# Residual block in float32 by split products: the "added" pair of a column block begun one pair ahead, and six, then eight seven-product pairs in the down projection

## Chip, cores, metric

The kernel runs on 1 core of one Trainium2 chip. The metric is the device time of one execution in microseconds. Three timed executions of the kernel before gave 1150.38, 1150.60 and 1150.38 us.

## What is computed

One layer over 256 tokens of width 2048, all in float32: a combined input projection, chunked softmax attention in eight heads, a gated recurrence (HGRN2) in eight heads, an output projection, and a SwiGLU block of inner width 5632. The change lies in the last part:

```python
    x = x + (mixed @ w_out[l]).astype(x.dtype)
    h2 = rmsnorm(x, norm2_gain[l])
    ff = jax.nn.silu(h2 @ w_gate[l]) * (h2 @ w_up[l])
    x = x + (ff @ w_down[l]).astype(x.dtype)
return rmsnorm(x, final_gain)
```

## The kernel before

**Split products.** A float32 product is made of three products in float32r: each operand is split in a high and a low half (`split`, L87: ScalarE copies to the high half, L88, and VectorE subtracts it from the source for the low half, L89), and TensorE forms high by high, high by low and low by high (`mul`, L699, matmul at L704). Weights are split on the chip as they arrive; high halves stand in tiles `wh`, low halves in `wl`, each a pool of four buffers.

**Pairs.** Gate and up are computed in 11 groups of 512 columns each (`Gated`, list `gated`), down in two groups (`Down`). A group goes over its contraction in pairs of 128-row blocks. Of each pair the four weight tiles (two row blocks by two outputs) come in one load of 1024 KB, and a pair is prepared (`prepare`) in one of three ways:

- `"d"`, ordinary: two halves of 128x1024 are split by ScalarE and VectorE, then 24 matmuls of 512 columns.
- `"s"`, seven-product: sums and differences of the tiles `ta` and `tb` are formed on VectorE (L747 to L749) and split too, so that seven instead of eight block products do, 21 matmuls. The sums of the left operand stand ready in `hs` (gate and up) or `sf` (down, made by `row_sums` from `fh` and `fl`).
- `"a"`, added: VectorE does nothing. `begin` (L711) loads the pair to `rawa` (one buffer), ScalarE writes its negated high half to `low` (L716, two halves of 128x1024, three buffers), and a DMA on GpSimd's queue adds the weights from memory onto it (L717), which leaves the low half. `prepare_begun` (L722) makes the high halves `wh` on ScalarE. Its 24 matmuls take the 16 with high halves first, and the 8 with `low` last.

A gated group after the first has the order of L879, `a4 s0 d5 s1 a6 s2 s3 d7`: 4 x 24 + 4 x 21 = 180 matmuls, and 8 transposes of 128x128. Group 0 has ordinary pairs alone. The last pair of a group is held and run output block by output block, so that VectorE and ScalarE can take each block as it ends.

**Order of work.** `run_groups` (L773) calls `prepare(i + 1)` and then runs the matmuls of the pair before it, so one pair is prepared while another runs; the order on each engine is settled by the scheduler from there. `prepare` also decides when an added pair begins: two pairs ahead if an ordinary pair comes between (a4 of the next group begins with s3), one pair ahead if a seven-product pair is followed by it (a6 begins with s1). All plain loads go through one queue, SP's, in program order (`dma`, L81, chains them): a load that waits for its buffer holds all that follow. Ordinary and seven-product pairs share three buffers `raw`.

**Down.** `order_of` (L765) lists a down group: some ordinary pairs first, then seven-product pairs with an ordinary one behind each, then the ordinary ones that are left. Group 0 has 7 ordinary pairs, 7 seven-product pairs with 6 ordinary ones between them, and 2 ordinary pairs at the end; group 1 has 1, then 8 seven-product pairs with ordinary ones between, and ordinary ones at the end. While the first ordinary pairs of group 0 run, `between` (L942) has `row_sums` make the four tiles of sums (each serves two seven-product pairs). Behind the last seven-product pair `spread` (L903) adds the products m1, m5, m6, m7 into the residual `x2`; behind the group `block` (L919) and `end` (L937) add and scale the output blocks.

Of the kernel before, what the change touches and what calls it, by code (L numbers as in the profile page):

```python
# [8 lines left out]
F32 = mybir.dt.float32  # L9
F32R = mybir.dt.float32r  # L10
I32 = mybir.dt.int32
AF = mybir.ActivationFunctionType
# [33 lines left out]
def hybrid_block(ctx: ExitStack, tc: tile.TileContext, x, xT, w_in, w_out, w_gu, w_down,  # L46
# [616 lines left out]
    def row_sums(dst, hi, lo):  # L663
        n = hi.shape[1] // 2
        a = dn.tile([P, 2, 2, S], F32, tag="ta", name="a")[:, 0:n]
        sm = dn.tile([P, 4, 2, P], F32, tag="tb", name="sm")[:, :, 0:n]
        nc.vector.tensor_tensor(a, hi.rearrange("p (j k) t -> p j k t", k=2).bitcast(F32),
                                lo.rearrange("p (j k) t -> p j k t", k=2).bitcast(F32), ALU.add)
        a11, a12, a21, a22 = a[:, :, 0, 0:P], a[:, :, 1, 0:P], a[:, :, 0, P:S], a[:, :, 1, P:S]
        nc.vector.tensor_tensor(sm[:, 0], a21, a22, ALU.add)  # L670
        nc.vector.tensor_tensor(sm[:, 1], sm[:, 0], a11, ALU.subtract)
        nc.vector.tensor_tensor(sm[:, 2], a11, a21, ALU.subtract)
        nc.vector.tensor_tensor(sm[:, 3], a12, sm[:, 1], ALU.subtract)
        split(dst[:, 0], dst[:, 1], sm)
# [8 lines left out]
    class Group:  # L683
# [25 lines left out]
            return load_chunk(self.src, self.base + j).rearrange("p (b n) -> p b n", n=W)  # L709

        def begin(self, j):  # L711
            raw, low = own["low"].tile([P, 4, W], F32, name="rawa"), []
            dma(raw.rearrange("p b n -> p (b n)"), self.src[self.base + j])
            for k in range(2):
                wl = own["low"].tile([P, 2, W], F32R, tag="low", name="low", bufs=3)
                tc.keep_in_program_order(nc.scalar.activation(wl, raw[:, 2 * k:2 * k + 2], AF.Copy, scale=-1.0))  # L716
                nc.gpsimd.dma_start(out=wl.rearrange("p b n -> p (b n)"),  # L717
                                    in_=self.src[self.base + j, :, 2 * k * W:2 * (k + 1) * W], accum_op=ALU.add)
                low.append(wl)
            self.begun = raw, low  # L720

        def prepare_begun(self, j):  # L722
            (raw, low), self.begun = self.begun, None
            tiles = []
            for k in range(2):
                wh = wsp.tile([P, 2 * W], F32R, tag="wh", name="wh")
                nc.scalar.activation(wh, raw[:, 2 * k:2 * k + 2].rearrange("p b n -> p (b n)"), AF.Copy)
                tiles.append([(wh[:, i * W:(i + 1) * W], low[k][:, i]) for i in range(2)])
            return [(f"c{t}{h}", self.lhs(2 * j + k, t), tiles[k][h if k == 0 else 1 - h], terms)
                    for terms in ((0, 2), (1,)) for k in range(2) for t in range(NT) for h in range(2)]  # L730
# [34 lines left out]
    def order_of(pairs, fast, lead, tail):  # L765
        slow = [j for j in range(pairs) if j not in fast]
        items = [("d", j) for j in slow[:lead]]
        mid = slow[lead:len(slow) - tail]
        for n, j in enumerate(fast):
            items += [("s", j)] + [("d", k) for k in mid[n:n + 1]]  # L770
        return items + [("d", j) for j in mid[len(fast):] + slow[len(slow) - tail:]]

    def run_groups(groups, following=None):  # L773
        todo = [(gr, n) for gr in groups for n in range(len(gr.items))]

        def prepare(i):
            kinds = [gr.items[n][0] for gr, n in todo[i:i + 3]]
            ahead = 2 if kinds[1:] == ["d", "a"] else 1 if kinds[0] == "s" and kinds[1:2] == ["a"] else 0
            if ahead:
                gr, n = todo[i + ahead]  # L780
                gr.begin(gr.items[n][1])
            gr, n = todo[i]
            return gr.prepare(*gr.items[n])

        steps, held = groups[0].ready or prepare(0), []
        for i, (gr, n) in enumerate(todo):
            ahead = None
            if n + 1 == len(gr.items):
                if i + 1 < len(todo):
                    ahead = prepare(i + 1)  # L790
                elif following is not None:
                    following.ready = following.prepare(*following.items[0])
                gr.run_blocks(held + steps, gr.block)
                held = []
                gr.end()
            elif n + gr.hold >= len(gr.items):
                held = held + steps
            else:
                gr.run(steps)
                seen = sum(1 for kind, _ in gr.items[:n + 1] if kind == "s")  # L800
                if gr.items[n][0] == "s" and seen == gr.ns:
                    gr.spread()
            if i + 1 < len(todo):
                steps = ahead or prepare(i + 1)
            gr.between(n)
# [28 lines left out]
    class Gated(Group):  # L834
# [31 lines left out]
        def between(self, n):  # L866
            if n == 0:
                if self.g == 0:
                    second_end()
                    for t in range(NT):  # L870
                        dma(x2d[t], x2[:, t, :])
                    own["hs"] = res.tile([P, 2, 4, FASTU, P], F32R, tag="res", name="hs")
                else:
                    ff_split(gated[self.g - 1].ff, self.g - 1)
            if self.g == 0 and 1 <= n <= (FASTU + 1) // 2:
                j0, j1 = 2 * n - 2, min(2 * n, FASTU)
                row_sums(own["hs"][:, :, :, j0:j1, :], h2[:, 2 * j0:2 * j1, 0, :], h2[:, 2 * j0:2 * j1, 1, :])
# [19 lines left out]
    class Down(Group):  # L897
# [39 lines left out]
        def end(self):  # L937
            if self.g == 0:
                for t, h in BLOCKS:
                    self.gained(t, h)  # L940

        def between(self, n):  # L942
            if self.g == 0:
                if n == 0:
                    gup.__exit__(None, None, None)
                    late = ctx.enter_context(tc.tile_pool(name="late", bufs=1))
                    own.update(f_last=late.tile([P, 2, 4, S], F32R, name="f_last"), fg=late.tile([P, D], F32, name="fg"))
                    ff_split(gated[-1].ff, len(gated) - 1)
                elif n <= FAST // 2:
                    ks = slice(4 * (n - 1), 4 * n)  # L950
                    row_sums(sf[:, n - 1], fh[:, ks, :], fl[:, ks, :])
                elif n == FAST // 2 + 1:
                    load_fg()
                if n == 2:
                    x2 = own["x2"] = res.tile([P, NT, D], F32, tag="res", name="x2")
                    for t in range(NT):
                        dma(x2[:, t, :], x2d[t])

    def finish(ps, t):
# [6 lines left out]
        for lo, hi in ((c0, c1), (c1, D)):  # L966
# [18 lines left out]
        nc.scalar.activation(x2[:, t, 1024:c0], x2[:, t, 1024:c0], AF.Copy, scale=r)  # L985
        dma(out[t, :, 1024:c0], x2[:, t, 1024:c0])

    down = [Down(g, order_of(KP, list(range(FAST - 1 + g)), 1 if g else 7, 2), w_down, g * KP, f_of, s_of)
            for g in range(2)]
    down[0].hold, down[1].hold = 1, 2  # L990
    run_groups(gated, down[0])
# [63 lines left out]
```

## Time and profile before

| | us |
|---|---|
| timed runs (3), median | 1150.38 |
| the profiled execution's own time | 1149.81 |
| its span, first to last instruction | 1148.1 |
| TensorE matmul busy (PE) | 1132.1 |
| TensorE weight load busy (PEld) | 943.9 |
| VectorE busy (DVE) | 914.5 |
| ScalarE busy (ACT) | 700.1 |

Times are of one profiled execution. The profile calls SyncE's queue SP and GpSimd POOL; "SPq" is a queue's issue of a DMA. A row of the view by windows gives a stretch, its length, and for each engine the busy time and the number of instructions. A row of the view in order of time gives start, duration, engine, line and operands, and in brackets how long the engine stood idle before it and what ended that. Matmuls overlap, so the time from one start to the next says more of TensorE's pace than the duration of one.

### The profile page before, as it was taken

Reading aid. Unit: us, or ns where it says so; the run is one execution under the profiler, and the core shown is the slowest. Engines: PE = TensorE matmul, PEld = TensorE weight load, DVE = VectorE, ACT = ScalarE, POOL = GpSimd, SP = SyncE. Lnnn points to the kernel's source line nnn. Section 1 sums busy time; section 2 is a strip of 40 time slices with the busy share of each in tenths; the row PEclk is TensorE's granted clock in tenths of the full one; section 3 lists DMA queues with packets and bytes.
Section 4 is the critical chain, followed back from the end, with each engine's and each line's share of the span. In section 5 each row is a group of like instructions: output and inputs, shape, how many; then the busy total and the mean of one; then the engine's idle time right before and its main releaser. Section 6 shows DMA issues by size and latency. Waiting matters only on the chain.

```text
span 1148.1 us, 14308 instructions
## 1 busy us (share of the span) xinstructions
PE 1132.1 (99%) x5381; PEld 943.9 (82%) x5381; DVE 914.5 (80%) x1166; ACT 700.1 (61%) x900; POOL 53.2 (5%) x73
## 2 busy tenths in 40 slices
PE   9999999999999999999999999999999999999996
PEld 7888888888888888888888788788788888878885
DVE  7577768947746666589889889889889998899885
ACT  7465656846645555576676676676676565555553
POOL 3200000000000000010010010010010000000000
PEclk9999999999999999999999999999999999999999
DMA  9655544554744547877886886886887765546552
GB/s 330 229 196 185 179 147 179 180 192 147 279 161 154 189 172 281 259 209 208 293 242 211 290 241 215 291 237 220 283 237 245 269 231 204 200 175 236 189 214 74
DMA packets 41397, 248.95 MB, mean 217 GB/s; under 512 B 4848, under 2 KB 5360, under 8 KB 15344
## 3 DMA queue, kind: packets, MB, share of 16 engines
q1 hardware_dynamic: 35568, 227.06, 53.5%
q0 software_dynamic: 5760, 20.97, 10.2%
q8 instruction: 42, 0.69, 0.2%
q14 instruction: 27, 0.22, 0.1%
HBM read 243.82 MB, written 4.19 MB: 216 GB/s over the span
## 4 chain that ended last, share of the span: by engine, by line
PE 87%; DVE 5%; ACT 3%; DMA 2%; issue 2%; ACTq 0%; SPq 0%; DVEq 0%
PE c L704 40%; PE acc L169 10%; PE m L704 10%; PE acc L171 5%; PE acc L144 5%; PE acc L146 5%; PE acc L145 5%; DVE wl L89 2%; ACT wh L88 2%; PE vps L144 1%; PE vps L145 1%; PE vps L146 1%; PE ptr L315 1%; DMA raw<-in_w_gu_dram 1%; DMA raw<-in_w_down_dram 1%
## 5 line engine op out<-in xcount | busy, mean ns | idle before, releaser
L89 DVE TENSOR_TENSOR wl<-raw,wh 128x1024 fp32r<-128x1024 f32 (+1 forms) x378 | 419.0, 1124 | 140.6 <-ACT wh L88 139.8
L88 ACT ACTIVATE wh<-raw 128x1024 fp32r<-128x1024 f32 (+1 forms) x378 | 362.1, 972 | 205.3 <-PE acc L146 75.2
L704 PE MATMUL c<-wh,h 128*128 128x512 f32 x928 | 277.0, 391 | 1.7 <-ACT wh L88 1.7
L704 PEld LDWEIGHTS c<-wh,h 128*128 128x128 f32 x928 | 173.5, 188 | 40.8 <-ACT wh L88 5.2
L169 PE MATMUL acc<-hx,wh 128*128 128x512 f32 x512 | 179.7, 395 | 0.0
L171 PE MATMUL acc<-hx,wl 128*128 128x256 f32 x512 | 142.6, 278 | 0.0
L704 PE MATMUL c<-wl,h 128*128 128x512 f32 x304 | 118.4, 389 | 0.2 <-DVE wl L89 0.2
L169 PEld LDWEIGHTS acc<-hx,wh 128*128 128x128 f32 x512 | 96.0, 188 | 21.7
L88 ACT ACTIVATE wh<-ta 128x1024 fp32r<-128x1024 f32 x55 | 58.3, 1061 | 73.6 <-DVE ta L747 34.9
L88 ACT ACTIVATE wh<-tb 128x1024 fp32r<-128x1024 f32 x55 | 58.3, 1060 | 63.0 <-PE c L704 32.6
L171 PEld LDWEIGHTS acc<-hx,wl 128*128 128x128 f32 x512 | 96.4, 188 | 0.1
L704 PE MATMUL c<-wh,fh 128*128 128x512 f32 x230 | 89.7, 390 | 0.2 <-DVE ff L853 0.2
L704 PE MATMUL c<-wh,fl 128*128 128x512 f32 x230 | 89.5, 389 | 0.0
L704 PE MATMUL c<-wl,fh 128*128 128x512 f32 x230 | 89.5, 389 | 0.0
L704 PE MATMUL m<-wh,hs 128*128 128x512 f32 x240 | 83.0, 392 | 1.3 <-ACT wh L88 1.3
L89 DVE TENSOR_TENSOR wl<-tb,wh 128x1024 fp32r<-128x1024 f32 x55 | 67.3, 1223 | 21.2 <-ACT wh L88 20.0
L89 DVE TENSOR_TENSOR wl<-ta,wh 128x1024 fp32r<-128x1024 f32 x55 | 67.2, 1222 | 15.0 <-ACT wh L88 14.9
L747 DVE TENSOR_TENSOR ta<-raw 128x1024 f32<-128x1024 f32 x55 | 67.3, 1223 | 10.6 <-DMA raw<-in_w_gu_dram 6.9
L717 POOL DMA_DIRECT2D low<-in_w_gu_dram x40 | 34.5, 871 | 730.5 <-ACT low L716 690.5
L704 PEld LDWEIGHTS c<-wl,h 128*128 128x128 f32 x304 | 57.1, 188 | 12.6 <-DVE wl L89 0.6
L704 PEld LDWEIGHTS m<-wh,hs 128*128 128x128 f32 x240 | 45.0, 188 | 12.8 <-ACT wh L88 3.7
L704 PEld LDWEIGHTS c<-wh,fh 128*128 128x128 f32 x230 | 43.2, 188 | 9.4 <-issue 0.6
(289 smaller groups left out, 1848.3 us busy)
## 6 DMA issues: line engine op xcount, KB each, us to landing
raw<-in_w_gu_dram SPq DMA_DIRECT2D x68, 1024.0 KB, 8.2
raw<-in_w_in_dram SPq DMA_DIRECT2D x48, 1024.0 KB, 4.8
raw<-in_w_down_dram SPq DMA_DIRECT2D x44, 1024.0 KB, 4.8
rawa<-in_w_gu_dram SPq DMA_DIRECT2D x20, 1024.0 KB, 5.2
low<-in_w_gu_dram POOLq DMA_DIRECT2D x40, 512.0 KB, 8.6
raw<-in_w_out_dram SPq DMA_DIRECT2D x16, 1024.0 KB, 4.8
raw<-in_w_in_dram SPq DMA_DIRECT2D x12, 512.0 KB, 6.0
raw<-in_w_in_dram SPq DMA_DIRECT2D x8, 256.0 KB, 4.6
```

Source lines behind the costliest of these rows:

```text
L88: nc.scalar.activation(hi, src, AF.Copy)
L89: nc.vector.tensor_tensor(lo, src, hi.bitcast(F32), ALU.subtract)
L144: nc.tensor.matmul(ps[t], lhsT=xh[:, tok], rhs=wh, start=kt == 0, stop=False)
L145: nc.tensor.matmul(ps[t], lhsT=xh[:, tok], rhs=wl, start=False, stop=False)
L146: nc.tensor.matmul(ps[t], lhsT=xl[:, tok], rhs=wh, start=False, stop=kt == kts - 1)
L169: nc.tensor.matmul(ps[m].rearrange("p j t -> p (j t)"), lhsT=wh[:, col], rhs=both, start=kt == 0, stop=False)
L171: nc.tensor.matmul(ps[m][:, 0, :], lhsT=wl[:, col], rhs=rhs[:, kt, 0, :], start=False, stop=kt == KD - 1)
L315: nc.tensor.transpose(pt[:, j, t, :], nat(t)[:, n0 + j * P:n0 + (j + 1) * P], ident)
L704: nc.tensor.matmul(self.bank[n], lhsT=a, rhs=b, start=self.left[n] == self.total[n], stop=self.left[n] == 1)
L717: nc.gpsimd.dma_start(out=wl.rearrange("p b n -> p (b n)"), in_=self.src[self.base + j, :, 2 * k * W:2 * (k + 1) * W], accum_op=ALU.add)
L747: nc.vector.tensor_tensor(ta, raw[:, 1:3], raw[:, 0:2], ALU.subtract)
```

## The change

Three things change.

1. An added pair begins always exactly one pair ahead. `begin` is cut in two: it loads `rawa`, and a new function `lower(k)` negates one half and issues its adding DMA. Ahead of a seven-product pair (a6 before s1) both halves come first, as they did. Ahead of an ordinary pair (a4 before d7 of the group ahead) the load and half 0 stand before that pair's own load and splits, and half 1 behind them; before, all of it stood ahead of s3, one pair earlier.
2. Down group 0 has 6 seven-product pairs in place of 7: 6 ordinary pairs, then six seven-product pairs each with an ordinary one behind it, then 4 ordinary ones. Its number of matmuls grows by 3. Group 1 keeps its order (8 seven-product pairs).
3. Only three tiles of sums are made in down group 0. The fourth is made in group 1, after its fifth pair; the load of the final gain comes one pair earlier.

```diff
         def begin(self, j):
-            raw, low = own["low"].tile([P, 4, W], F32, name="rawa"), []
+            raw = own["low"].tile([P, 4, W], F32, name="rawa")
             dma(raw.rearrange("p b n -> p (b n)"), self.src[self.base + j])
-            for k in range(2):
-                wl = own["low"].tile([P, 2, W], F32R, tag="low", name="low", bufs=3)
...
-            self.begun = raw, low
+            self.begun = j, raw, []
+
+        def lower(self, k):
+            j, raw, low = self.begun
+            wl = own["low"].tile([P, 2, W], F32R, tag="low", name="low", bufs=3)
+            tc.keep_in_program_order(nc.scalar.activation(wl, raw[:, 2 * k:2 * k + 2], AF.Copy, scale=-1.0))
+            nc.gpsimd.dma_start(out=wl.rearrange("p b n -> p (b n)"),
+                                in_=self.src[self.base + j, :, 2 * k * W:2 * (k + 1) * W], accum_op=ALU.add)
+            low.append(wl)
...
         def prepare(i):
-            kinds = [gr.items[n][0] for gr, n in todo[i:i + 3]]
-            ahead = 2 if kinds[1:] == ["d", "a"] else 1 if kinds[0] == "s" and kinds[1:2] == ["a"] else 0
-            if ahead:
-                gr, n = todo[i + ahead]
-                gr.begin(gr.items[n][1])
             gr, n = todo[i]
-            return gr.prepare(*gr.items[n])
+            nxt, m = todo[i + 1] if i + 1 < len(todo) else (None, 0)
+            begins = nxt is not None and nxt.items[m][0] == "a"
+            if begins:
+                nxt.begin(nxt.items[m][1])
+                nxt.lower(0)
+                if gr.items[n][0] == "s":
+                    nxt.lower(1)
+            steps = gr.prepare(*gr.items[n])
+            if begins and gr.items[n][0] == "d":
+                nxt.lower(1)
+            return steps
...
+        def sum_round(self, i):
+            ks = slice(4 * i, 4 * i + 4)
+            row_sums(sf[:, i], fh[:, ks, :], fl[:, ks, :])
+
         def between(self, n):
+            if self.g == 1 and n == 4:
+                self.sum_round(FAST // 2 - 1)
...
-                elif n <= FAST // 2:
-                    ks = slice(4 * (n - 1), 4 * n)
-                    row_sums(sf[:, n - 1], fh[:, ks, :], fl[:, ks, :])
-                elif n == FAST // 2 + 1:
+                elif n < FAST // 2:
+                    self.sum_round(n - 1)
+                elif n == FAST // 2:
                     load_fg()
...
-    down = [Down(g, order_of(KP, list(range(FAST - 1 + g)), 1 if g else 7, 2), w_down, g * KP, f_of, s_of)
+    down = [Down(g, order_of(KP, list(range(FAST if g else FAST - 2)), 1 if g else 6, 2), w_down, g * KP, f_of, s_of)
```

What stands on the engines, at the end of one gated group and the start of the next. On SP's queue before, from the load of s2 of one group to that of s0 of the next:

```order
L85 DMA raw_4389<-in_w_gu_dram 128x2048
L85 DMA rawa_4433<-in_w_gu_dram 128x2048
L85 DMA raw_4441<-in_w_gu_dram 128x2048
L85 DMA raw_4492<-in_w_gu_dram 128x2048
L85 DMA raw_4566<-in_w_gu_dram 128x2048
```

Here 4389 is s2, 4433 a4, 4441 s3, 4492 d7, 4566 s0. In the changed kernel the same place reads s2 (4389), s3 (4433), a4 (4484), d7 (4489), s0 (4566):

```order
L85 DMA raw_4389<-in_w_gu_dram 128x2048
L85 DMA raw_4433<-in_w_gu_dram 128x2048
L85 DMA rawa_4484<-in_w_gu_dram 128x2048
L85 DMA raw_4489<-in_w_gu_dram 128x2048
L85 DMA raw_4566<-in_w_gu_dram 128x2048
```

The load of s3 and that of a4 have changed places.

On ScalarE before, from the last split of s2 (wh<-tb, first row) to the high halves of a4 (wh<-rawa); the copy ff<-m begins the group's spread:

```order
L88 ACTIVATE wh<-tb 128x1024
L716 ACTIVATE low<-rawa 128x1024 x2
L88 ACTIVATE wh<-raw 128x512
L88 ACTIVATE wh<-raw 128x1024
L88 ACTIVATE wh<-ta 128x1024
L842 COPY ff<-m_4603 128x512
L88 ACTIVATE wh<-tb 128x1024
L88 ACTIVATE wh<-raw 128x1024 x2
L727 ACTIVATE wh<-rawa 128x1024 x2
```

And in the changed kernel, from and to the same places:

```order
L88 ACTIVATE wh<-tb 128x1024
L88 ACTIVATE wh<-raw 128x512
L88 ACTIVATE wh<-raw 128x1024
L88 ACTIVATE wh<-ta 128x1024
L88 ACTIVATE wh<-tb 128x1024
L849 COPY ff<-m_4603 128x512
L719 ACTIVATE low<-rawa 128x1024
L88 ACTIVATE wh<-raw 128x1024 x2
L719 ACTIVATE low<-rawa 128x1024
L729 ACTIVATE wh<-rawa 128x1024 x2
```

The two negated halves have gone from ahead of s3's four splits to both sides of d7's two (wh<-raw 128x1024 x2).

On TensorE in the changed kernel, the first matmuls of d7 behind s3 (wh_4844 and wh_4848 are the high halves of its two parts, wl_4845 and wl_4849 the low ones):

```order
L704 MATMUL c10_4540<-wh_4805,h2_3174 128x512
L704 MATMUL c00_4538<-wh_4844,h2_3174 128x512
L704 MATMUL c00_4538<-wl_4845,h2_3174 128x512
L704 MATMUL c00_4538<-wh_4844,h2_3174 128x512
L704 MATMUL c00_4538<-wh_4848,h2_3174 128x512
L704 MATMUL c01_4539<-wh_4844,h2_3174 128x512
L704 MATMUL c01_4539<-wl_4845,h2_3174 128x512
L704 MATMUL c01_4539<-wh_4844,h2_3174 128x512
L704 MATMUL c01_4539<-wh_4848,h2_3174 128x512
L704 MATMUL c10_4540<-wh_4844,h2_3174 128x512
L704 MATMUL c00_4538<-wl_4849,h2_3174 128x512
```

The first low half is used by d7's second matmul and the second by its tenth; before, three matmuls of s3 and of d7 were mixed at this place, and the low half of m6's weights came behind d7's first two.

More of the change, by code (lines that the diff above doesn't have):

```diff
@@ L711, in begin @@
         def begin(self, j):
-            raw, low = own["low"].tile([P, 4, W], F32, name="rawa"), []
+            raw = own["low"].tile([P, 4, W], F32, name="rawa")
             dma(raw.rearrange("p b n -> p (b n)"), self.src[self.base + j])
-            for k in range(2):
-                wl = own["low"].tile([P, 2, W], F32R, tag="low", name="low", bufs=3)
[L716 to L719, printed above, removed]
-            self.begun = raw, low
+            self.begun = j, raw, []
[6 more added lines that the diff above has]
+            low.append(wl)
         def prepare_begun(self, j):
-            (raw, low), self.begun = self.begun, None
+            (_, raw, low), self.begun = self.begun, None
             tiles = []
```

## The prediction

> **What bounds the kernel now.** I read the page first, then the view by windows over single gated groups, then the order of time on the engines where a group is longer than it need be.
>
> ```profile
> span 1148.1 us, 14308 instructions
> PE 1132.1 (99%) x5381; PEld 943.9 (82%) x5381; DVE 914.5 (80%) x1166; ACT 700.1 (61%) x900; POOL 53.2 (5%) x73
> ```
>
> TensorE is busy for 99% of the span, but its matmuls overlap, so waits hide in that figure. Stretches that start and end at the same matmul of a group or pair show them. The rows are: gated group 1; groups 2 to 9 together; two groups alone; then three stretches of down.
>
> ```profile
> core 0: us, PE busy (x) PEld busy (x) DVE busy (x) ACT busy (x) POOL busy (x), PEclk, DMA share, GB/s
> 489.11:530.82 41.71, 41.71 (x189) 34.61 (x189) 36.61 (x43) 28.49 (x32) 3.44 (x4) 1.00 0.74 229
> 530.82:871.26 340.44, 337.43 (x1505) 275.65 (x1505) 305.09 (x352) 231.73 (x265) 27.49 (x32) 1.00 0.79 247
> 573.15:615.41 42.26, 42.05 (x190) 34.47 (x189) 38.20 (x45) 28.95 (x34) 3.44 (x4) 1.00 0.79 249
> 615.41:658.28 42.87, 42.29 (x189) 34.46 (x189) 38.16 (x45) 28.86 (x34) 3.42 (x4) 1.00 0.79 245
> 946.08:956.28 10.20, 10.20 (x47) 8.45 (x46) 8.83 (x10) 5.83 (x7) 0.00 (x0) 1.00 0.67 239
> 1007.28:1040.14 32.86, 31.85 (x140) 25.75 (x139) 31.84 (x38) 18.52 (x26) 0.00 (x0) 1.00 0.48 174
> 1050.34:1081.69 31.35, 30.90 (x137) 25.26 (x136) 26.33 (x28) 17.47 (x19) 0.00 (x0) 1.00 0.57 205
> ```
>
> A seven-product pair and an ordinary one, 21 + 24 = 45 matmuls, take 10.20 us without a wait: 0.2267 us for each start, at a granted clock of 1.00. Group 1 takes 41.71 us with the same work as the others. Groups 2 to 9 take 340.44 us, and eight times 41.71 is 333.68: 6.76 us are waits, some 0.55 in one group and 1.16 in the next. VectorE has 38.2 us to do in 42.3, so it isn't the bound by its sum; something comes late. In down, 1007.28 to 1040.14 holds 138 matmuls, 31.28 us at that pace, so 1.58 us are waits, and 1050.34 to 1081.69 holds 135, 30.60 us, so 0.75.
>
> Where does a group wait? In order of time, the end of the group that ends near 735 us:
>
> ```profile
> 719.84 2.01 ACT L716 ACTIVATE low<-rawa 128x1024 fp32r<-128x1024 f32 x2 [0.19 <-DMA rawa<-in_w_gu_dram]
> 722.33 1.22 DVE L747 TENSOR_TENSOR ta<-raw 128x1024 f32<-128x1024 f32 x1 [1.42 <-DMA raw<-in_w_gu_dram]
> 726.94 0.69 DVE L749 TENSOR_TENSOR tb<-raw,tb 128x512 f32<-128x512 f32 x1
> 727.72 1.06 ACT L88 ACTIVATE wh<-tb 128x1024 fp32r<-128x1024 f32 x1 [1.34 <-DVE tb L749]
> 728.69 2.00 ACT L88 ACTIVATE wh<-raw 128x1024 fp32r<-128x1024 f32 x2
> 728.83 0.50 PE L704 MATMUL m<-wh,hs 128*128 128x512 f32 x1 [0.36 <-ACT wh L88]
> 729.78 0.73 PE L704 MATMUL c<-wh,h 128*128 128x512 f32 x2 [0.22 <-ACT wh L88]
> 713.92 0.33 SPq L85 DMA_DIRECT2D rawa<-in_w_gu_dram  x1
> 714.34 13.68 SPq L85 DMA_DIRECT2D raw<-in_w_gu_dram  x4
> SPq L85 <- ACT wh L727: 176.1, 19, 16.9
> DVE ta L747 <- DMA raw<-in_w_gu_dram: 6.9, 8, 1.7
> ```
>
> Read from below. The queue SP stands before `rawa` until ScalarE has read the last added pair (L727: 19 times, up to 16.9 us), and only then, in one burst from 713.92 on, come a4's `rawa` and the loads of s3, d7 and s0. So s3's weights land late, VectorE waits for them (8 times, 6.9 us, one for each of the eight groups), `tb` is ready at 727.63, ScalarE splits it at 727.72, and the matmul that needs it waits; d7's split stands behind that on ScalarE, and TensorE waits again.
>
> **The part of gate and up: a4 begun one pair later.** The load of s3 goes ahead of `rawa`, and has only to wait for its own buffer. The trace has a case of this: the last group has no a4 behind it, so nothing stands ahead of its s3.
>
> ```profile
> 895.60 0.39 PE L704 MATMUL m<-wh,h 128*128 128x512 f32 x1
> 895.84 1.06 ACT L88 ACTIVATE wh<-tb 128x1024 fp32r<-128x1024 f32 x1 [0.30 <-PE c L704]
> 897.28 2.98 ACT L88 ACTIVATE wh<-raw 128x1024 fp32r<-128x1024 f32 x3
> 898.37 2.36 DVE L89 TENSOR_TENSOR wl<-raw,wh 128x1024 fp32r<-128x1024 f32 x2 [0.21 <-ACT wh L88]
> 900.58 0.39 PE L704 MATMUL c<-wl,h 128*128 128x512 f32 x1
> 901.26 0.39 PE L704 MATMUL c<-wl,h 128*128 128x512 f32 x1
> ```
>
> Call 895.60, s3's first matmul, zero. `tb` is split at +0.24, released by TensorE and not by VectorE; d7's high halves start at +1.68; its low halves are done at about +4.0 and +5.13. TensorE uses them at +4.98 and +5.66 and waits for neither: 1.0 and 0.5 us of cover. The change puts one negated half, 1.05 us, ahead of d7's two splits. That moves the low halves to +5.05 and +6.2. The first is then used at 21 x 0.2267 + 0.2267 = +4.99, so 0.06 us late. The second is used by d7's tenth matmul now, at +6.80, so it is in time. So the cover just about holds; if it is gone altogether, a group loses up to 1.05 - 0.5 = 0.55 us, which is what the better groups lose today. I take 0.15 a group, between 0 (group 1 and the last) and 0.55, near the former by this count. Eight groups then gain 6.76 - 8 x 0.15 = 5.56 us (6.76 at best, 2.36 at 0.55).
>
> **What the moved halves meet.** The half `low` is needed when 45 + 16 matmuls are over, at +13.83, and the second half four matmuls later, at +14.74. Its DMA follows the copy:
>
> ```profile
> L716 ACT ACTIVATE low<-rawa x40: 1038/1045/1062, 461.2 to 875.0; 128x1024 fp32r<-128x1024 f32 x40
> DMA to landing us min/median/max: 5.3/8.6/13.4
> 721.30 1.80 POOL L717 DMA_DIRECT2D low<-in_w_gu_dram  x2 [14.73 <-ACT low L716]
> low<-in_w_gu_dram POOLq DMA_DIRECT2D x2, 512.0 KB, 10.2
> q1 hardware_dynamic: 212, 1.61, 101.2%
> low<-in_w_gu_dram POOLq DMA_DIRECT2D x2, 512.0 KB, 6.3
> ```
>
> The issue comes 0.4 us behind the first copy's end (719.84 + 1.05 to 721.30). So half 0, copied from +1.68 to +2.73, issues at +3.1, and half 1, copied behind d7's two high halves from +4.7 to +5.75, at +6.15. The last three rows are two pairs of issues: at 678.7 they took 10.2 us in the median, since for 4.3 us, to 683.0, only queue q1 (the plain loads) moved anything, at 101% of the engines; at 704.7, with no load ahead, 6.3. In the change s0's load is issued as soon as s2's buffer is read, long before zero, and d5's at about zero; the next `rawa` waits for a4's own high halves (to +7.7). So half 1 meets a nearly empty queue, lands at about +12.5 and has 2.3 us to spare; at the overall median of 8.6 it would land at +14.75, just when it is needed.
>
> [...]
>
> **Down.** One seven-product pair fewer is 3 matmuls more: 3 x 0.2267 = +0.68 us, all on TensorE. [...]
>
> In return the crowd at the end of group 0 dissolves. It stands now as follows in the chain that ended last:
>
> ```profile
> 1025.94 1.74 DVE wl L89 x2
> 1027.67 1.15 DVE ta L747
> 1030.36 1.07 ACT wh L88
> 1031.47 1.42 PE m L704 x5
> ```
>
> VectorE does the spread and the block sums of group 0 up to 1025.94 and begins group 1's s0 only then; its `ta` is ready at 1028.8 and TensorE waits 1.58 us in that stretch. With four ordinary pairs more between the last s and the group's end instead of two, the spread's adds are over by then, and `ta` of s0 stands ahead of the block sums on VectorE. I take 0.2 of the 1.58 as left: -1.38 (0 to -1.58).
>
> The fourth round of sums moves into group 1, where less time is free:
>
> ```profile
> L667 DVE TENSOR_TENSOR a<-fh,fl 128x1024 f32<-128x1024 f32 x4 | 4.9, 1222 | 0.1
> L89 DVE TENSOR_TENSOR sf<-sm,sf 128x1024 fp32r<-128x1024 f32 x4 | 4.9, 1220 | 0.0
> L673 DVE TENSOR_TENSOR sm<-a,sm 128x256 f32<-128x256 f32 x4 | 1.7, 424 | 0.0
> ```
>
> A round is 1.22 + 4 x 0.42 + 1.22 = 4.1 us. A couple of pairs leaves VectorE 10.20 - 8.83 = 1.4 us, so the round is made up over three couples, from the lead that VectorE has, and it borrows the buffers `ta` and `tb`, for which s3's sums queue. Nearest row: where VectorE lost time in 1050.34 to 1081.69, TensorE lost 0.75. I take +0.2, from 0 to 0.75. The 0.75 itself stays.
>
> **Sum.** -5.56 + 0.68 - 1.38 + 0.2 = -6.06 us. The profiled execution took 1149.81 us (span 1148.1 and 1.7 around it), so 1143.75; the median of the timed runs is 0.57 above it, so **1144.3 us**. At best -6.76 + 0.68 - 1.58 = -7.66, and if the 0.75 goes too, 1142.0.
>
> **Rivals.**
>
> *The first half of `low` uncovers d7's split* (0.13). ScalarE is in order, and the copy stands ahead of d7's high halves; had `rawa` or TensorE released it later than I count, each of eight groups would lose the 0.55 of today's better groups. -2.36 - 0.5 = -2.86 gives 1147.5, with a little more wait 1148.3. For it: the cover is used up within 0.1 us. Against: the second low half is used 1.1 us later than before.
>
> *`low` lands too late* (0.10), the case on the slower side. It decides from 8.6 us between issue and landing of half 1; up to there nothing is lost. At the 10.2 of the pair that queued, TensorE waits 1.6 us in front of a4's low products in nine groups: +14.4 - 6.1, 1158.7 us. The gain is eaten at 8.6 + 6.06 / 9 = 9.3. For it: 13.4 has been measured, and the slack of today's early start is given up. Against: those that took long queued behind the burst of loads, which this change breaks up.
>
> *The change doesn't do what it says* (0.09): s3's load now waits for another thing (the DMA of a6's low halves, or its buffer), VectorE starts as late as before, and only down changes by -0.5: 1149.9. Against it: the last group.
>
> **How the numbers follow.** The forecast has 0.68 (its own range 1142.0 to 1146.5). With the first rival the range is 1142.0 to 1148.3, which leaves out 0.19. What can be told from no change is 0.2%, 2.3 us, so faster is below 1148.1: the forecast and most of the first rival, 0.78; the same 0.12; slower 0.10.
>
> **What would show it.** Right: in the new profile the stretch of eight gated groups is near 335 us, VectorE's wait for raw at `ta` is gone there, `tb`'s split is released by TensorE, and TensorE has no wait before the `low` products. Wrong: groups of 42.3 us or more; a wait of TensorE on the adding DMA at the end of each added pair; s3's `ta` still ended by a DMA; or new waits in down group 1 around its third and fourth seven-product pair.

## The result, and the profile after

The changed kernel takes 1143.26 us in the median of five timed runs (1142.53 to 1146.05), the kernel before 1150.38 (1148.68 to 1150.60, five runs): a ratio of 0.9946, 95% interval 0.9930 to 0.9962. The prediction was 1144.3, with a range of 1142.0 to 1148.3. The profiled execution took 1142.54 us against 1149.81.

From the page of the changed kernel:

```profile
span 1140.8 us, 14295 instructions
PE 1128.7 (99%) x5384; PEld 944.1 (83%) x5384; DVE 912.4 (80%) x1161; ACT 698.4 (61%) x898; POOL 53.5 (5%) x73
```

The view by windows of the changed kernel, with the same limits in the program as before: gated group 1, groups 2 to 9 together, two groups alone; then a seven-product pair and an ordinary one in down group 1, right behind the moved round of sums; and all of down, from the start of its first matmul to that of the last matmul of the kernel.

```profile
core 0: us, PE busy (x) PEld busy (x) DVE busy (x) ACT busy (x) POOL busy (x), PEclk, DMA share, GB/s
488.24:530.10 41.86, 41.86 (x189) 34.57 (x189) 36.09 (x42) 28.52 (x32) 3.44 (x4) 1.00 0.76 226
530.10:865.15 335.05, 335.05 (x1505) 276.43 (x1505) 307.91 (x353) 232.08 (x265) 27.50 (x32) 1.00 0.82 251
571.99:613.90 41.91, 41.91 (x190) 34.57 (x189) 38.49 (x45) 29.01 (x34) 3.43 (x4) 1.00 0.81 251
613.90:655.79 41.89, 41.89 (x189) 34.54 (x189) 38.48 (x45) 29.01 (x34) 3.42 (x4) 1.00 0.82 251
1052.76:1063.40 10.64, 10.64 (x47) 8.29 (x45) 10.44 (x12) 6.66 (x7) 0.00 (x0) 1.00 0.55 199
900.03:1131.42 231.39, 231.39 (x1022) 190.84 (x1022) 198.90 (x228) 126.64 (x144) 0.00 (x0) 1.00 0.56 202
```

And the same stretch of down in the kernel before:

```profile
906.14:1138.63 232.49, 231.02 (x1018) 190.20 (x1019) 203.26 (x233) 128.40 (x146) 0.00 (x0) 1.00 0.55 201
```

Groups 2 to 9 went from 340.44 to 335.05 us, 5.39 less; 42.26 and 42.87 in turn have become 41.9 each. Down takes 1.10 less and group 1 takes 0.15 more. Group 1 starts 0.87 earlier (its first seven-product pair at 487.30 us against 488.17), of which 0.83 was there at the first matmul of gate and up (435.96 against 436.79), ahead of all that the change touches. Together that is -7.21 of the -7.27.

Rows picked from the view in order of time, at the end of a gated group of the changed kernel:

```profile
660.82 0.33 SPq L85 DMA_DIRECT2D raw<-in_w_gu_dram  x1
669.11 0.33 SPq L85 DMA_DIRECT2D rawa<-in_w_gu_dram  x1
...
674.34 1.22 DVE L749 TENSOR_TENSOR ta<-raw 128x1024 f32<-128x1024 f32 x1
...
680.11 0.39 PE L704 MATMUL m<-wh,h 128*128 128x512 f32 x1
680.36 1.06 ACT L88 ACTIVATE wh<-tb 128x1024 fp32r<-128x1024 f32 x1 [0.30 <-PE c L704]
681.79 1.06 ACT L719 ACTIVATE low<-rawa 128x1024 fp32r<-128x1024 f32 x1
682.75 1.99 ACT L88 ACTIVATE wh<-raw 128x1024 fp32r<-128x1024 f32 x2
683.26 0.84 POOL L720 DMA_DIRECT2D low<-in_w_gu_dram  x1 [21.46 <-ACT low L719]
683.83 1.23 DVE L89 TENSOR_TENSOR wl<-raw,wh 128x1024 fp32r<-128x1024 f32 x1 [1.15 <-ACT wh L88]
684.64 1.05 ACT L719 ACTIVATE low<-rawa 128x1024 fp32r<-128x1024 f32 x1
685.11 0.50 PE L704 MATMUL c<-wl,h 128*128 128x512 f32 x1
685.45 0.86 PE L704 MATMUL c<-wh,h 128*128 128x512 f32 x3
...
686.10 0.86 POOL L720 DMA_DIRECT2D low<-in_w_gu_dram  x1 [2.00 <-ACT low L719]
687.61 0.33 SPq L85 DMA_DIRECT2D rawa<-in_w_gu_dram  x1
...
694.10 1.07 PE L704 MATMUL c<-low,h 128*128 128x512 f32 x4
```

The load of s3 is issued at 660.82, 8.3 us ahead of a4's `rawa` (669.11). VectorE begins `ta` at 674.34 and waits for nothing, and the split of `tb`, 0.25 us behind s3's first matmul (680.11), is released by TensorE. The low half of d7's first part is ready at 683.83 + 1.23 = 685.06, and TensorE uses it at 685.11. The adding DMA of half 1 goes out at 686.10, 1.5 us ahead of the next `rawa`; it landed 5.86 us later, at 691.96. TensorE takes the first `low` at 694.10, with no wait. In the view of the tile `low` of the changed kernel:

```profile
DMA to landing us min/median/max: 5.3/6.6/11.1
```

It was 5.3/8.6/13.4.

### The profile page after: what moved, and what is told of

It is laid out like the page before. It is cut to its first block, busy times and chain, and to the rows that moved or that the text cites. A ratio compares the mean times of both kernels' runs of the same rounds, so it can differ in the third digit from the quotient of the medians.

```text
span 1140.8 us, 14295 instructions
## 1 busy us (share of the span) xinstructions
PE 1128.7 (99%) x5384; PEld 944.1 (83%) x5384; DVE 912.4 (80%) x1161; ACT 698.4 (61%) x898; POOL 53.5 (5%) x73
## 4 chain that ended last, share of the span: by engine, by line
PE 94%; DVE 2%; ACT 1%; DMA 1%; issue 0%; SPq 0%; ACTq 0%
PE c L704 45%; PE m L704 13%; PE acc L169 10%; PE acc L171 5%; PE acc L144 5%; PE acc L146 5%; PE acc L145 5%; PE vps L145 1%; PE ptr L315 1%; PE vps L146 1%; PE vps L144 1%; DVE wl L89 1%; DMA x2d<-x 1%; ACT wh L88 0%; DMA raw<-in_w_in_dram 0%
## 5 line engine op out<-in xcount | busy, mean ns | idle before, releaser
L704 PE MATMUL c<-wh,h 128*128 128x512 f32 x928 | 273.7, 390 | 0.0
L704 PE MATMUL c<-wh,fh 128*128 128x512 f32 x236 | 92.1, 390 | 0.2 <-DVE ff L860 0.2
L704 PE MATMUL c<-wh,fl 128*128 128x512 f32 x236 | 91.9, 389 | 0.0
L704 PE MATMUL c<-wl,fh 128*128 128x512 f32 x236 | 91.9, 389 | 0.0
```

Source lines behind the costliest of these rows:

```text
L704: nc.tensor.matmul(self.bank[n], lhsT=a, rhs=b, start=self.left[n] == self.total[n], stop=self.left[n] == 1)
```

## The experiments

The theory: a4's early `rawa` held s3's load in SP's queue, so the gain lies in the order of the loads; the place of the two negated halves on ScalarE has only to do no harm, between d7's split, which they delay, and the landing of the adding DMAs, which they delay too. The rivals: the copies' own place on ScalarE gave the gain; down gave it; a half of `low` uncovers d7 or lands too late.

All medians, and the ratios against the kernel before, which was timed anew along with each set: its median was 1149.12 beside e1 to e4, 1149.32 beside e5 to e8 and 1149.77 beside e9 to e11. So a run is compared by its ratio, not by its median against 1150.38.

| kernel | median us | ratio, 95% interval | groups 2 to 9 | down |
|---|---|---|---|---|
| before | 1150.38 | | 340.44 | 232.49 |
| changed | 1143.26 | 0.9946, 0.9930 to 0.9962 | 335.05 | 231.39 |
| e1 gated part alone | 1143.96 | 0.9957, 0.9943 to 0.9972 | 335.00 | 231.76 |
| e2 down alone | 1149.04 | 0.9997, 0.9988 to 1.0007 | 340.60 | 231.38 |
| e3 s3's load first, nothing else | 1144.62 | 0.9964, 0.9949 to 0.9978 | 335.74 | 231.74 |
| e4 copies later, nothing else | 1173.32 | 1.0213, 1.0198 to 1.0228 | 365.46 | 231.72 |
| e5 both halves behind d7's parts | 1159.53 | 1.0088, 1.0075 to 1.0102 | 346.96 | 231.81 |
| e6 both halves ahead of them | 1149.00 | 0.9998, 0.9989 to 1.0008 | 340.12 | 231.89 |
| e7 an a4's halves behind its own highs | 1237.65 | 1.0771, 1.0756 to 1.0785 | 409.21 | 231.30 |
| e8 fourth round of sums in group 0 | 1144.54 | 0.9963, 0.9951 to 0.9976 | 334.93 | 233.12 |
| e9 first half ahead of s3's splits | 1144.90 | 0.9960, 0.9947 to 0.9974 | 335.91 | 231.57 |
| e10 seven ordinary pairs first | 1143.06 | 0.9945, 0.9932 to 0.9959 | 335.10 | 230.85 |
| e11 e9 and e10 together | 1144.69 | 0.9956, 0.9943 to 0.9968 | 335.86 | 231.59 |

The last two columns are rows of the view by windows, from one profile each.

### The two parts alone (e1, e2)

e1 is the changed kernel with down as it was, e2 the kernel before with the changed down. Of e1's edit, the line that gives group 0 its seventh seven-product pair back (the fourth round of sums goes back to group 0 with it):

```diff
-    down = [Down(g, order_of(KP, list(range(FAST if g else FAST - 2)), 1 if g else 6, 2), w_down, g * KP, f_of, s_of)
+    down = [Down(g, order_of(KP, list(range(FAST - 1 + g)), 1 if g else 7, 2), w_down, g * KP, f_of, s_of)
```

> The added pairs begin as in the change; down is as before (7, then 8 seven-product pairs, four rounds of sums in group 0). My theory: the two parts add up, so gated groups 2 to 9 take about 335 us (340.44 before, 335.06 with the change) and everything behind the last gated group 242.0 as before; about 5.4 us below the kernel before. Rival: part of the gain in gate and up comes only because down starts otherwise, or the down part carries most of the gain; then this run stays within 2 us of the kernel before.

> Down is as in the change; the added pairs begin as before. My theory: groups 2 to 9 stay at 340.4 us, and the part from the last gated group to the end goes from 242.0 to about 240.8 as in the change: 3 matmuls more, and the waits of 1.58 and 0.75 us gone; about 1.2 us below the kernel before. Rival, as the prediction had it: -0.5 us, since the 0.75 stays and the moved round of sums costs.

The gated part alone gives all that timing can tell; down alone can't be told from no change.

### Which half of the gated part (e3, e4)

e3 is the kernel before, but a pair's own load goes out ahead of `begin` of the added pair behind it; both copies still stand ahead of s3's splits:

```diff
-        def prepare(self, kind, j):
+        def prepare(self, kind, j, begin=None):
...
             raw = self.load(j)
+            if begin:
+                begin()
...
```

> The kernel before, with one thing moved: the load of s3 goes to the queue ahead of the a4 load. The two negated halves stay ahead of the splits of s3 on ScalarE, one pair earlier than in the change. Theory that the place in the load queue is the cause: VectorE no longer waits for the weights of s3, groups 2 to 9 take 335 to 336.5 us, 4 to 5.4 us gained. Rival, that the two copies of 1.05 us ahead of the four splits of s3 are the cause: groups stay at 42.3 us or more, 338.5 to 340.

In groups 2 to 9 it takes 335.74 us, so 4.70 of the 5.39 us come from the order of two loads in one queue.

e4 leaves the loads and moves the copies alone, behind the splits of s3:

```diff
-                gr, n = todo[i + ahead]
-                gr.begin(gr.items[n][1])
+                nxt, m = todo[i + ahead]
+                nxt.begin(nxt.items[m][1])
...
-            return gr.prepare(*gr.items[n])
+            steps = gr.prepare(*gr.items[n])
+            if ahead == 2:
+                nxt.lower(0)
+                nxt.lower(1)
+            return steps
...
```

> The kernel before, with the other thing moved: the two negated halves of a4 come behind the four splits of s3 on ScalarE; the a4 load stays ahead of that of s3 in the queue. Theory of the load queue: the weights of s3 land as late as before, groups 2 to 9 stay at 339.5 to 341 us, perhaps more since the copies now stand ahead of the splits of d7. Rival, the copies: 335 to 337 us.

It is slower by 2%, which neither the theory (339.5 to 341 us for groups 2 to 9, "perhaps more") nor the rival had: 365.46. With s3's load still late, the copies now stand between its late splits and those of d7. TensorE waits at d7's low half, and what follows is not at full pace. The view in order of time, then that by windows:

```profile
744.89 1.20 PE L704 MATMUL c<-wh,h 128*128 128x512 f32 x4 [0.39 <-ACT wh L88]
747.28 0.73 PE L704 MATMUL c<-wl,h 128*128 128x512 f32 x1 [1.19 <-DVE wl L89]
```

```profile
747.28:750.57 3.29, 3.29 (x8) 2.61 (x9) 1.68 (x2) 0.40 (x1) 0.00 (x0) 0.52 1.05 203
```

Eight matmuls in 3.29 us are 0.41 each, at a granted clock of 0.52: the clock had fallen, though no single wait was longer than 1.4 us. It fell so in three groups alone, at 0.2 us for each of some eight matmuls: about 5 of the 25 us that e4 loses in groups 2 to 9. The rest is waits. So to delay the copies is no gain in itself. They may stand late only because s3's load is early.

### Where the halves may stand (e5, e6, e7, e9)

```diff
 e5: both behind d7's parts
                 nxt.begin(nxt.items[m][1])
-                nxt.lower(0)
                 if gr.items[n][0] == "s":
+                    nxt.lower(0)
                     nxt.lower(1)
             steps = gr.prepare(*gr.items[n])
             if begins and gr.items[n][0] == "d":
+                nxt.lower(0)
                 nxt.lower(1)
```

> The changed kernel, but of an a4 both negated halves stand behind the two high halves of d7's parts on ScalarE, not one on each side. In the changed kernel TensorE still waits some 0.11 us at d7's second matmul, and a group takes 41.88 us in place of 41.72. Theory (what is left is the 1.05 us copy ahead of d7's split, the cover being just used up): d7's low halves are ready 1 us earlier, that wait goes, a group takes 41.72 to 41.75, groups 2 to 9 take 333.8 to 334.1 in place of 335.05, and the time is 1142.1, about 1.1 below the changed kernel. Half 0 is issued some 2 us later and still lands before +13.8. Rival A (the rest of the wait has another cause): groups stay at 41.9 and the time at 1143.2. Rival B (two adding DMAs issued together share the queue and land too late): waits in front of the low products of a4, 1145 or more.

Rival B of these, and dearer than it said: 1159.53. d7's split is uncovered no more, but half 1 comes too late. The rows: the issue of the two halves, that of the next load of an added pair, and TensorE:

```profile
692.37 1.81 POOL L720 DMA_DIRECT2D low<-in_w_gu_dram  x2 [23.66 <-PE c L704]
694.84 0.33 SPq L85 DMA_DIRECT2D rawa<-in_w_gu_dram  x1
704.44 0.72 PE L704 MATMUL c<-low,h 128*128 128x512 f32 x2 [2.10 <-DMA low<-in_w_gu_dram]
```

Half 1 goes out at 693.32, 5.99 us behind s3's first matmul (687.33), exactly as in the changed kernel, and again 1.5 us ahead of the next `rawa`. But half 0 went out only 0.95 us before it, and landed at 697.95. By then the plain loads had begun to move. The queues from 698 to 702, in the view of DMA of that window (packets, MB, share of the engines):

```profile
q1 hardware_dynamic: 104, 0.85, 55.5%
q0 software_dynamic: 96, 0.36, 46.6%
```

In that window the adding DMA (q0) and the loads (q1) share the engines, 46.6% to 55.5%, and half 1 takes 11.08 us in place of 5.86. It lands at +17.06, counted from s3's first matmul, where +14.74 is needed: 2.3 us late, and TensorE starts that matmul 2.3 us late. Half 0 ahead of d7's split has a second use that the prediction hadn't seen. In the changed kernel half 0 has landed by 688.61, and half 1 has the queue to itself while the next load, though issued at 687.61, still moves nothing. The views of DMA from the issue of `rawa` on, 687.61 to 690.5 in the changed kernel and 694.84 to 697.5 in e5, show q0, and of the plain loads nothing:

```profile
q0 software_dynamic: 135, 0.49, 99.2%
```

```profile
q0 software_dynamic: 138, 0.50, 105.1%
```

In both kernels the plain load begins to move at about +10.7. By then the two halves have moved 1.03 of their 1.05 MB in the changed kernel and 0.64 in e5, where the rest shares.

```diff
 e6: both ahead of d7's parts
                 nxt.lower(0)
-                if gr.items[n][0] == "s":
-                    nxt.lower(1)
+                nxt.lower(1)
             steps = gr.prepare(*gr.items[n])
-            if begins and gr.items[n][0] == "d":
-                nxt.lower(1)
```

> The changed kernel, but of an a4 both negated halves stand ahead of d7's two high halves. Theory (a copy ahead of d7's split is paid in full once the cover is gone): d7's low halves come at about +6.1 and +7.3 behind s3's first matmul. The scheduler has put four high products ahead of the first low one, which is then used at +5.7, so TensorE waits 0.4 to 0.5 us a group, eight groups lose 3 to 4 us, and the time is 1146 to 1147. Rival (VectorE and TensorE have more room there than I counted, the copy costs nothing): 1143 to 1143.5. Rival (as where the kernel before had both copies ahead of s3's splits): no matter, since their place on ScalarE costs nothing as long as s3's load is early.

```profile
687.36 1.22 DVE L89 TENSOR_TENSOR wl<-raw,wh 128x1024 fp32r<-128x1024 f32 x1
688.63 0.50 PE L704 MATMUL c<-wl,h 128*128 128x512 f32 x1 [0.34 <-DVE wl L89]
```

As the theory had it in kind, and somewhat more in size than its 0.4 to 0.5 us a group: TensorE starts d7's first low half 0.51 us late, and a group takes 42.51 in place of 41.88. Nine groups at 0.63 are 5.7 us, the whole gain: the ratio is 0.9998. The low half is ready 1.22 us later than in the changed kernel (688.58, +6.17, against +4.95): the second copy's 1.05 us, and a sum of the group's spread that VectorE did first. The scheduler hid a part: it uses the low half three matmuls later, 0.68 us. The rest is paid.

```diff
 e7: the halves of an a4 behind its own high halves
         def prepare_begun(self, j):
-            (_, raw, low), self.begun = self.begun, None
+            _, raw, low = self.begun
...
                 nc.scalar.activation(wh, raw[:, 2 * k:2 * k + 2].rearrange("p b n -> p (b n)"), AF.Copy)
+                highs.append(wh)
+            while len(low) < 2:
+                self.lower(len(low))
...
             if begins:
                 nxt.begin(nxt.items[m][1])
-                nxt.lower(0)
                 if gr.items[n][0] == "s":
+                    nxt.lower(0)
                     nxt.lower(1)
...
```

> The changed kernel, but the two negated halves of every added pair come behind the pair's own high halves on ScalarE, so that their adding DMAs are issued some 3 us later; nothing else moves. This tests the point from which low lands too late. Theory (the DMA takes about 5.9 us when the queue is empty, and TensorE waits for what is beyond the need at +13.8 and +14.7 behind s3's first matmul): issued at about +9 and +10 they land at +15 to +16, TensorE waits about 1.2 us in front of the low products of an added pair, 19 of them, some 23 us in all, 1166; if matmuls start further apart behind such waits, as where s3's splits stood behind the copies, some 5 to 15 more. Rival (the DMA takes the 8.6 us that it had as the median in the kernel before): the wait is near 4 us a pair and the time near 1220. Rival (the break-even is further off): under 1150.

The run does less than the expectation says. It moves the halves of an added pair only where an ordinary pair stands ahead, which are the ten a4; behind a seven-product pair (a6) both halves still go out early, as in the changed kernel. TensorE waits 20 times in the profile, twice for each of the ten. So at the expectation's own price of 1.2 us a pair the run should have cost 12 us, and at its rival's 4 us a pair 40.

The direction is right and the size isn't: 1237.65, 94 us more. The expectation let the DMA run in an empty queue and took 5.9 us for it; in e7 the adding DMAs took 10.0 us in the median and 15.4 at most. I put that down to the next load, which can go out once ScalarE has read `rawa` and would then share the engines with the halves; that is my estimate, and no view here shows the two queues apart. The view of the tile `low`:

```profile
DMA to landing us min/median/max: 8.4/10.0/15.4
```

TensorE waits twice for a pair, here in order of time and then by windows:

```profile
693.07 1.36 PE L704 MATMUL c<-low,h 128*128 128x512 f32 x4 [2.08 <-DMA low<-in_w_gu_dram]
698.06 1.19 PE L704 MATMUL c<-low,h 128*128 128x512 f32 x2 [3.63 <-DMA low<-in_w_gu_dram]
```

```profile
690.46:693.87 3.41, 1.32 (x7) 0.76 (x5) 3.34 (x5) 1.66 (x2) 0.00 (x0) 1.00 1.03 305
693.87:704.11 10.24, 6.61 (x20) 5.10 (x19) 3.03 (x4) 2.58 (x4) 0.00 (x0) 0.50 0.58 205
```

Counted from the start that was due, the two waits are 2.3 and 4.0 us, of the 9.3 by which a group grew (51.15 in place of 41.88). The granted clock is 0.50 from 693.87 to 704.11, from right behind the first wait on, so the matmuls behind the second are slow as well as late.

e9 has `begin` and half 0 of an a4 called from s3's `prepare`, as e3 does, and half 1 behind d7's parts:

```diff
+                def early():
+                    after_next.begin(after_next.items[k][1])
+                    after_next.lower(0)
...
-            steps = gr.prepare(*gr.items[n])
+            steps = gr.prepare(*gr.items[n], early)
...
```

> The changed kernel, but of an a4 half 0 is negated ahead of s3's four splits on ScalarE (s3's load still ahead of that of a4), and half 1 stays behind d7's two parts; nothing stands between s3's last split and d7's. It asks again, without a late adding DMA, whether the 0.15 us a group that is left is the copy ahead of d7's split. Theory (it is; and ScalarE's waits for TensorE between s3's splits, 0.73, 0.35 and 0.30 us, take the 1.05 us copy in): d7's low halves are ready 1 us ahead of their use, half 1 is issued at about +5.3 behind s3's first matmul and, with no half 0 ahead of it in the queue, lands at about +11; a group takes 41.72, groups 2 to 9 take 333.8, and the time is 1142.0, 1.2 below the changed kernel. Rival A (the copy delays s3's splits instead, as both copies did there at 41.96 us a group): 41.85 to 42.0, 1143.3 or more. Rival B (half 1 shares the queue with the next load of an added pair and lands too late): a wait in front of the low products of a4, 1145 or more.

Rival A, though not for its reason. s3's splits are as early as ever, TensorE's stop at d7 is gone, and half 1 lands 5.5 us behind its issue; but two other short stops of 0.11 us have come, in a4's high products and in s0's, and a group takes 42.0. So the 0.11 us at d7 was the copy, as the theory said, and yet there is nothing to be had by moving it ahead of s3.

### Down (e8, e10, e11)

```diff
 e8: the fourth round of sums in group 0, as before
-            if self.g == 1 and n == 4:
-                self.sum_round(FAST // 2 - 1)
...
-                elif n < FAST // 2:
+                elif n <= FAST // 2:
                     self.sum_round(n - 1)
...
```

> The changed kernel, but the fourth round of sums is made in down group 0 with the other three, as in the kernel before; the six and eight seven-product pairs stay. Theory (the moved round costs 0.36 us, two waits in group 1 at its second seven-product pair, where VectorE has little time free): these waits go, from down's first matmul to the end it takes 231.0 in place of 231.4, and the time is about 1142.9, not to be told from the changed kernel by timing. Rival (in group 0 the round comes in the way of the first seven-product pairs): 231.4 or more.

The rival: 233.12. With six ordinary pairs ahead, the first seven-product pair comes while VectorE is still at the sums, and `tb` is late (view in order of time):

```profile
936.93 1.06 ACT L88 ACTIVATE wh<-tb 128x1024 fp32r<-128x1024 f32 x1 [2.68 <-DVE tb L751]
938.04 0.50 PE L704 MATMUL m<-wh,sf 128*128 128x512 f32 x1 [0.70 <-ACT wh L88]
```

So the moved round is not a by-product of the six pairs; with six ordinary pairs ahead it is needed. e10 is e8 with the ordinary pair put back at the head:

```diff
-    down = [Down(g, order_of(KP, list(range(FAST if g else FAST - 2)), 1 if g else 6, 2), w_down, g * KP, f_of, s_of)
+    down = [Down(g, order_of(KP, list(range(FAST if g else FAST - 2)), 1 if g else 7, 2), w_down, g * KP, f_of, s_of)
```

> The changed kernel, but down group 0 has seven ordinary pairs, not six, ahead of its six seven-product pairs (three instead of four ordinary ones stay at its end), and the fourth round of sums is made in group 0. The same number of matmuls. Theory (the round in group 0 cost 1.9 us because with six ordinary pairs ahead the seven-product pairs come one pair sooner than the sums have room for; three ordinary pairs are enough at the end): from down's first matmul to the end 231.0, the 0.36 us in group 1 gone; time 1142.9. Rival A (the crowd at the end of group 0 is back): 231.4 to 232.5. Rival B (the round in group 0 costs whatever stands ahead): 233.

Down takes 230.85 us, 0.54 less than in the changed kernel, with no wait of a seven-product pair left; 231.0 was expected. Its median, 1143.06, is the lowest of all, but can't be told from 1143.26.

> The edits of the two kernels before together: half 0 of an a4 ahead of s3's splits, half 1 behind d7's parts; seven ordinary pairs at the head of down group 0 with all four rounds of sums. If both theories hold, groups 2 to 9 take 333.8 and down 231.0 us, and the time is 1141.6, some 1.6 below the changed kernel; if only the first holds 1142.0, only the second 1142.9, none 1143.3 or more.

e11 has e10's down to the letter and takes 231.59. The rows of one place in both, `ta` of group 1's third seven-product pair, in e11 and in e10:

```profile
1066.09 1.23 DVE L751 TENSOR_TENSOR ta<-raw 128x1024 f32<-128x1024 f32 x1 [2.01 <-DMA raw<-in_w_down_dram]
```

```profile
1065.71 1.23 DVE L749 TENSOR_TENSOR ta<-raw 128x1024 f32<-128x1024 f32 x1
```

The load took 7.04 us in e11 and 4.69 in e10. This is the 0.75 us of the kernel before: there the load of the same place took 7.1. In the view of DMA, from 1064 to 1066 in the kernel before:

```profile
q8 instruction: 1, 0.02, 3.0%
raw<-in_w_down_dram SPq DMA_DIRECT2D x1, 1024.0 KB, 7.1
```

A packet of the queue that the view names instruction (q8) lies within 0.7 us of the issue of a load near that place in all thirteen profiles. That load took 4.7 to 5.2 us in seven of them and 5.7 to 7.1 in six. TensorE lost 0.5 to 0.75 us there in four of them (before, e5, e6, e11) and 0.2 or nothing in the others. That this packet is what delays the load isn't shown, and why the load is late in one execution and not in the next stays open.

## Why the prediction was right

**The place and the cause: right, and shown.** The load of s3 behind `rawa` was the wait. e3 undoes that alone and gets 4.70 of 5.39 us; e4 moves the copies alone, and groups 2 to 9 take 25 us more. The other 0.69 us is what the later copies add once the load is early.

**The cover at d7: right to a tenth, one count short.** Forecast: low half ready at +5.05, used at +4.99, 0.15 us lost in each of eight groups. Measured: ready at +4.95, used at +5.00, and a group takes 41.88 where 41.71 is free of waits, so 0.17: the stop itself is 0.11, and the next dozen matmuls follow each other at 0.230 us in place of 0.227, which is the rest. What was left out is group 1, which now has an added pair behind it that is begun in the same way: it went from 41.71 to 41.86. The gated part gave 5.24 us over nine groups (5.39 - 0.15), and 5.56 was forecast.

**The landing of `low`: right.** Issue of half 1 at +5.99 (forecast +6.15), landing at +11.85 (+12.45), use of the second half at +14.9. So there were 3.0 us to spare, not 2.3. The point from which it decides was right as well: e5 lets it land at +17.06, and TensorE is 2.3 us late.

**Down: the sum was near, its terms were not.** Forecast +0.68 - 1.38 + 0.2 = -0.5. The moved round costs about 0.45, not 0.2: the two pairs behind it take 10.64 us, where 45 matmuls without a wait take 10.20, and e10, which has neither the moved round nor the six ordinary pairs, takes 230.85 in all against 231.39. The row that the 0.2 was taken from, the 0.75, was a late load and not VectorE's lack of time. The wait at the end of group 0 went altogether: the old down without the late load takes 231.74 (e3; 231.76 and 231.72 in e1 and e4), so 231.74 + 0.68 - 230.85 = 1.57 of the 1.58. In sum 231.39 - 231.74 = -0.35. That the two misses went opposite ways, and so left the sum near, was luck.

**"The 0.75 itself stays": wrong.** I took a wait of one execution for part of the kernel. The old down has it in the profile of the kernel before and not in e1, e3 and e4. It makes the profiled executions differ by 0.75 more than the kernels do, and with the 0.87 us ahead of group 1 it is why the profile showed -7.27 against the forecast's -6.06. (In the profiles of all kernels, which hardly differ up to there, the first matmul of gate and up starts between 435.8 and 438.9 us.) The kernels' own part is nearer -5.24 - 0.35 = -5.6. The medians differ by 7.1, with an interval of 4.4 to 8.1 (0.9930 to 0.9962 of 1150.38); against the three later medians of the kernel before, 1149.12 to 1149.77, the changed kernel's 1143.26 is 5.9 to 6.5 lower.

**The rivals.** The first half uncovering d7 was priced at up to 0.55 a group; with a second copy ahead, in e6, 0.63 a group is paid on top. `low` landing too late did not come true, but the spare hangs on more than I counted: delaying half 0 by d7's two splits, with half 1 at the same place, brought it about in e5, at 1159.53, near the 1158.7 that this rival was priced at. I looked at half 1's own issue alone, and not at what stands ahead of it in its own queue.

**Two queues with work at once.** In the kernel before, `low` moved nothing for 4.3 us from 678.7 on while the plain loads had 101% of the engines; from 683 to 686 both moved, the adding DMAs at 80.9% and the loads at 24.9%. In the changed kernel half 1 shared with nothing for most of its way, since the next `rawa` moved nothing for 3.2 us behind its issue while the adding DMAs had 99.2%. In e5 the plain loads moved nothing for about 3.2 us while the adding DMAs had 105%, and from 698 to 702 the two queues shared, 46.6% to 55.5%. So at these three places the queue that came second moved nothing for 3.2 to 4.3 us, and behind that both moved. What held it for that time isn't shown.

## What to carry to other kernels

A prefetch that is begun early can cost more than it saves if it waits for its buffer in a queue that later, more urgent loads must pass (here 4.70 us over eight groups, by e3): look at what stands behind a waiting issue, and put the one that is needed first ahead. When a DMA is moved later, ask not only when it is issued, but what is ahead of it in its queue and which load will share the engines before it is done (in e5 half 1 took 11.08 us in place of 5.86). And before a small wait in one profile enters a sum, look for it in another execution (the 0.75 us of the kernel before was not there in e1, e3 and e4).

## What the runs showed of the hardware

**TensorE's clock fell behind two short waits in e4, and not behind a longer one in e5.** In e4 the granted clock fell to 0.50 at 747.38 for 3.41 us, in e7 at 693.87 for 10.24. The view by windows, two stretches of 3.41 us of e4, the second of them that at 0.50, and then two of e5 around its wait for half 1:

```profile
743.97:747.38 3.41, 1.83 (x8) 0.87 (x6) 3.26 (x5) 3.41 (x4) 1.08 (x2) 1.00 0.97 217
747.38:750.79 3.41, 3.41 (x8) 2.65 (x9) 1.58 (x2) 0.30 (x1) 0.00 (x0) 0.50 1.02 197
```

```profile
700.13:703.54 3.41, 2.21 (x10) 1.50 (x8) 3.34 (x4) 1.06 (x1) 0.00 (x0) 1.00 1.03 363
703.54:706.95 3.41, 2.51 (x15) 2.21 (x16) 2.68 (x4) 1.91 (x3) 0.00 (x0) 1.00 1.01 387
```

In e4 two waits of 0.55 and 1.36 us lie in the first stretch, with matmuls in 1.83 of its 3.41 us; in the second the clock is 0.50, with matmuls 427 ns apart in place of 227. In e5 the wait of 2.3 us lies across the end of the first stretch, with matmuls in 2.21 us of the first and 2.51 us of the second, and the clock is 1.00 in both. In e7 the first wait, of 2.3 us too, lies within the 3.41 us ahead of the fall, which hold matmuls for 1.32 us. What sets the clock isn't shown.

**A stop cost 0.11 us at d7 of the changed kernel, where hardly anything was waited for.** The matmul at 685.11 started on time (its low half was ready at 685.06), lasted 0.50 in place of 0.39, and the next began 0.34 us behind it in place of 0.227. The dozen behind it are 0.230 apart in the mean. The same 0.34 stands behind the longer waits in e4 (742.05 to 742.39) and e6 (688.63 to 688.97).
